# The up-projection of an MLP by Strassen's scheme: seven products of half width in place of eight, in seven of eight groups

## The chip, the cores and the metric

The kernel runs on one core of a Trainium2 chip. The metric is device microseconds (us) of one execution. A measurement takes the median of several runs; the profile is one further execution with the hardware profiler on.

TensorE (PE in the profile) multiplies matrices: a weight load puts a block of 128x128 into the array, then a matmul streams up to 512 columns past it and adds into PSUM. VectorE (DVE) and ScalarE (ACT) work on tiles element by element and can read PSUM; GpSimd (POOL) works on tiles in SBUF; SyncE (SP) issues most of the DMAs. Each engine takes its instructions in order and waits for others on semaphores.

## The reference

A decoder trunk of two layers over 512 tokens of width 1024. Each layer mixes tokens by three attentions, then applies an MLP:

```python
for l in range(DEPTH):
    h = rmsnorm(x, g_mix[l])
...
    x = x + merged @ w_out[l]
    u = rmsnorm(x, g_mlp[l]) @ w_mlp1[l]
    x = x + jnp.square(jax.nn.relu(u)) @ w_mlp2[l]
```

`w_mlp1` is 1024x4096, `w_mlp2` 4096x1024, and everything is float32. The change is in the last two lines.

## The kernel before, in words

All activations are kept transposed, features on the 128 partitions and the 512 tokens along the free axis: x is eight tiles of 128x512 (`s["x"]`), one for each 128 of the 1024 features.

**Three matmuls for one.** A float32 operand is split into a high part (a copy rounded to the matmul's type, by ACT) and a low part (the difference, by DVE): `split_into`, L100 to L102. `mm3` (L108 to L111) adds high times high, high times low and low times high into the same PSUM bank. So each product of a 128x128 weight block and 512 tokens is three matmuls of 512 columns, each with its own weight load.

**The program and its weights.** `layer` builds a list of entries. An entry is a function that issues one piece of work, with the weight units that it needs; a unit is at most 1024 elements on each partition, 512 KB. Behind all layers, the last loop (L926 to L938) walks through the list: before each entry it loads units ahead by SP's queue into `wraw` (3 buffers, `RB`) and splits them into `whi` and `wlo` (4 buffers each, `NB`), in the order in which they are used. A split is one ACT and one DVE instruction of 128x1024 (L101, L102). The framework takes this order as the priority in which it places instructions on the engines, may interleave entries that do not depend on each other, and sets the semaphores.

**The stages of a layer.** Projections and attentions come first, as a planned mix (`PLAN`), then `y8_item` (8 entries), `out_item` (8 entries: the merged output, the addition to x, and `feed`, which scales x by the MLP's gain, splits it into `s["h2"]`, and adds x squared into a running tile), and then the MLP. The factor 1/rms of each token isn't in `h2`: `row_stats` (L241) works it out from the squares, behind the last out item, by small matmuls and a power on POOL, and broadcasts it as `R2` over the partitions. It is applied to u.

**The MLP before.** The 4096 hidden features are four quarters of eight blocks of 128. `u_item(qr, j)` (L833) makes one block: 8 k x 3 matmuls of 512 columns into a bank of `ps_s`, then DVE takes relu times `R2` (L839), ACT squares it twice, once into the high part (L841) and once in place (L842), and DVE subtracts for the low part (L843). `w2_item(qr, ft)` (L847) adds a quarter's share to one of the eight output tiles: 8 k x 3 matmuls into a bank of `ps_acc`, then DVE adds it to x (L853). In the last quarter the output tile is final: it is stored to `out`, or in layer 0 fed to the next layer and stored for it. The order is written out in L902: `u(0) + u(1) + d(0) + u(2) + d(1) + u(3) + d(2) + d(3)`.

**Buffers.** Tiles of 128x512 come from pools: `H` (16) for h, the merged output and the even quarters of u, `O` (16) for `h2` among others, `B` (24) for much in the attentions and the odd quarters of u, `scr` (5) for scratch, `P` (3, of 128x1024) for the attentions' probabilities. PSUM has 2 banks `acc`, 3 `s`, 2 `tp` and 1 `o`.

Of the kernel before, what the change touches and what calls it, by code (L numbers as in the profile page):

```python
# [37 lines left out]


class Entry:  # L40
    def __init__(self, fn, units=()):
        self.fn, self.units = fn, list(units)


def merge(att, gemm):
# [14 lines left out]
def tile_trunk(ctx: ExitStack, tc: tile.TileContext, x_t, mem_t, mem_n, pos, ifr, gcol, grow, w_ck, w_cq, w_kvb, w_qb,  # L60
# [10 lines left out]
    pw_raw, pw_hi, pw_lo = pool("wraw", RB), pool("whi", NB), pool("wlo", NB)  # L71
# [10 lines left out]
    def tl(which, dt=F32):  # L82
        return pools[which].tile([P, 512], dt, tag=which, name=nm(which))
# [197 lines left out]
    def layer(l):  # L281
# [14 lines left out]
        def begin():  # L296
            if l == 0:
                sqs = new_sqs()
                h = []
                xts = []  # L300
                for k in range(KT):
                    xt = tl("X")
                    nc.sync.dma_start(out=xt, in_=x_t[k * P:(k + 1) * P, :])
                    xts.append(xt)
                    if k in (0, 2, 5):
                        load_raw()
                for k, xt in enumerate(xts):
                    h.append(feed(0, k, xt, C_MIX, "H", sqs))
                st["h"], st["sqs"] = h, sqs
            s["h"] = st["h"]  # L310

# [492 lines left out]
        def y8_item(ft):  # L804
            def fn(w):
                q = ps("s")
                for k in range(KT):
                    mm3(q, (w[0][0][:, k, :], w[0][1][:, k, :]), s["od"][k], k == 0, k == KT - 1)
                y_mix(q, 0, ft, False)
                hi, lo = tl("H", F32R), tl("H", F32R)  # L810
# [22 lines left out]
        def u_item(qr, j):  # L833
            def fn(w):
                q = ps("s")
                for k in range(KT):
                    mm3(q, (w[0][0][:, k, :], w[0][1][:, k, :]), s["h2"][k], k == 0, k == KT - 1)
                z = tl("scr")
                V.scalar_tensor_tensor(out=z, in0=q, scalar=0.0, in1=s["R2"], op0=ALU.max, op1=ALU.mult)  # L839
                hi, lo = (tl("H" if qr % 2 == 0 else "B", F32R) for _ in range(2))  # L840
                A.activation(out=hi, in_=z, func=AF.Square)  # L841
                A.activation(out=z, in_=z, func=AF.Square)  # L842
                V.tensor_tensor(out=lo, in0=z, in1=hi, op=ALU.subtract)  # L843
                s.setdefault(("u", qr), []).append((hi, lo))
            return Entry(fn, [w_1[l, qr * 8 + j]])

        def w2_item(qr, ft):  # L847
            def fn(w):
                q = ps("acc")
                for k in range(KT):  # L850
                    mm3(q, (w[0][0][:, k, :], w[0][1][:, k, :]), s["u", qr][k], k == 0, k == KT - 1)
                xt = s["x"][ft]
                V.tensor_tensor(out=xt, in0=q, in1=xt, op=ALU.add)  # L853
                if qr < 3:
                    return
                if l == L - 1:
                    nc.sync.dma_start(out=out[ft * P:(ft + 1) * P, :], in_=xt)
                    return
                if ft == 0:
                    st["sqs"], st["h"] = new_sqs(), []  # L860
                st["h"].append(feed(l + 1, ft, xt, C_MIX, "H", st["sqs"]))
                nc.sync.dma_start(out=xs_dram[ft * P:(ft + 1) * P, :], in_=xt)
            return Entry(fn, [w_2[l, qr, ft]])

        def gy4(w_o, key, b, first):
            r = []
# [33 lines left out]
        u = lambda q: [u_item(q, j) for j in range(8)]  # L900
        d = lambda q: [w2_item(q, ft) for ft in range(KT)]
# [6 lines left out]
    units = [ap for e in prog for ap in e.units]  # L908
    raws, splits = [], []
    consumed = 0  # L910

    def load_raw():
        ap = units[len(raws)]
        a, b = ap.shape[1], ap.shape[2]
        t = pw_raw.tile([P, 1024], F32, tag="wraw", name=nm("wraw"))
        nc.sync.dma_start(out=t[:, :a * b].rearrange("p (a b) -> p a b", a=a), in_=ap)
        raws.append((t, a, b))

    def do_split():
        t, a, b = raws[len(splits)]  # L920
        hi = pw_hi.tile([P, 1024], F32R, tag="whi", name=nm("whi"))
        lo = pw_lo.tile([P, 1024], F32R, tag="wlo", name=nm("wlo"))
        split_into(hi[:, :a * b], lo[:, :a * b], t[:, :a * b])
        splits.append(tuple(z[:, :a * b].rearrange("p (a b) -> p a b", a=a) for z in (hi, lo)))

    for i, e in enumerate(prog):  # L926
        if i == 0:
            e.fn([])
            continue
        while len(splits) < min(len(units), consumed + NB):  # L930
            while len(raws) < min(len(units), len(splits) + RB):
                load_raw()
            do_split()
        while len(raws) < min(len(units), len(splits) + RB):
            load_raw()
        n = len(e.units)
        e.fn(splits[consumed:consumed + n])
        consumed += n  # L938
# [6 lines left out]
def _layout(np, i):  # L945
# [54 lines left out]
    d["w_1"] = each(lambda l: blk(i["w_mlp1"][l], P))  # L1000
    d["w_2"] = each(lambda l: np.stack([blk(i["w_mlp2"][l][q * 1024:(q + 1) * 1024], P) for q in range(4)]))
    return d


# [20 lines left out]
```

## Time and profile before

| | us |
|---|---|
| median of 3 runs (2017.49 to 2018.43) | 2017.84 |
| the profiled execution | 2019.04 |
| its span, first to last instruction | 2017.2 |
| layer 0: start to the end of the out items | 0 to about 667 |
| layer 0: MLP | about 667 to 1017.5 |
| layer 1: MLP | about 1663 to 2017.2 |

How to read it: a page gives the share of the span in which each engine was busy, and the chain of work that ended last, followed back from the last instruction. A group row has line, engine, operation, out<-in by tile names, shapes, count, then busy us in total and mean ns of one, then the idle time before them and what ended it. A window row has busy time and number of instructions of PE, PEld (weight loads), DVE, ACT and POOL in a stretch of the span, then the granted TensorE clock (1.00 is full), the DMA share and GB/s. A timeline row has start, duration, engine, line, operation and tiles. A matmul's duration in it runs to its modelled end and overlaps the next ones; what one costs in a stream is the distance between starts.

### The profile page before, as it was taken

Reading aid. Unit: us, or ns where it says so; the run is one execution under the profiler, and the core shown is the slowest. Engines: PE = TensorE matmul, PEld = TensorE weight load, DVE = VectorE, ACT = ScalarE, POOL = GpSimd, SP = SyncE. Lnnn points to the kernel's source line nnn. Section 1 sums busy time; section 2 is a strip of 40 time slices with the busy share of each in tenths; the row PEclk is TensorE's granted clock in tenths of the full one; section 3 lists DMA queues with packets and bytes.
Section 4 is the critical chain, followed back from the end, with each engine's and each line's share of the span. In section 5 each row is a group of like instructions: output and inputs, shape, how many; then the busy total and the mean of one; then the engine's idle time right before and its main releaser. Section 6 shows DMA issues by size and latency. Waiting matters only on the chain.

```text
span 2017.2 us, 27896 instructions
## 1 busy us (share of the span) xinstructions
PE 1976.3 (98%) x10880; PEld 1711.2 (85%) x10880; DVE 1187.2 (59%) x2235; ACT 961.9 (48%) x1855; POOL 155.7 (8%) x153
## 2 busy tenths in 40 slices
PE   8999999999999999999999999999999999999999
PEld 7778989888888888888888899988888888888887
DVE  7756677687745443434447667678777554434442
ACT  5766765555533432323347667556555333323321
POOL 0300101111100000000002001011111000000000
PEclk9989999999999999999999999999999999999999
DMA  5233222222224333333332321221222333333332
GB/s 170 73 107 105 64 64 69 69 71 66 74 76 149 92 102 94 94 100 100 114 109 65 124 86 53 72 76 63 63 74 74 115 115 94 95 95 101 97 94 73
DMA packets 54676, 181.06 MB, mean 90 GB/s; under 512 B 6417, under 2 KB 7441, under 8 KB 54545
## 3 DMA queue, kind: packets, MB, share of 16 engines
q1 hardware_dynamic: 51840, 175.66, 28.1%
q10 hardware_dynamic: 2704, 3.62, 0.6%
q8 instruction: 86, 1.41, 0.3%
q14 instruction: 46, 0.37, 0.1%
HBM read 175.06 MB, written 4.19 MB: 89 GB/s over the span
## 4 chain that ended last, share of the span: by engine, by line
PE 91%; DVE 5%; ACT 2%; issue 1%; DMA 1%; POOL 0%; ACTq 0%; DVEq 0%; POOLq 0%
PE psacc L109 19%; PE psacc L110 19%; PE psacc L111 19%; PE pss L111 7%; PE pss L109 7%; PE pss L110 7%; PE pss L625 2%; PE pso L654 2%; PE pss L622 2%; PE pstp L666 1%; PE pstp L650 1%; DVE wlo L102 1%; PE pso L110 1%; PE pso L111 1%; PE pso L109 1%
## 5 line engine op out<-in xcount | busy, mean ns | idle before, releaser
L101 ACT ACTIVATE whi<-wraw 128x1024 fp32r<-128x1024 f32 (+3 forms) x320 | 334.4, 1046 | 694.3 <-PE psacc L110 353.8
L102 DVE TENSOR_TENSOR wlo<-wraw,whi 128x1024 fp32r<-128x1024 f32 (+3 forms) x320 | 386.0, 1206 | 94.1 <-ACT whi L101 92.0
L109 PE MATMUL psacc<-H,whi 128*128 128x512 f32 x816 | 321.0, 393 | 3.7 <-DVE G L781 3.2
L110 PE MATMUL psacc<-H,whi 128*128 128x512 f32 x816 | 319.1, 391 | 0.0
L111 PE MATMUL psacc<-H,wlo 128*128 128x512 f32 x816 | 319.0, 391 | 0.0
L109 PE MATMUL psacc<-whi,H 128*128 128x256 f32 (+1 forms) x928 | 270.3, 292 | 11.9 <-ACT whi L101 6.9
L110 PE MATMUL psacc<-wlo,H 128*128 128x256 f32 (+1 forms) x928 | 266.4, 287 | 0.9 <-DVE wlo L102 0.9
L111 PE MATMUL psacc<-whi,H 128*128 128x256 f32 (+1 forms) x928 | 265.5, 288 | 0.0
L110 PE MATMUL pss<-O,whi 128*128 128x512 f32 x640 | 249.2, 389 | 0.0
L111 PE MATMUL pss<-O,wlo 128*128 128x512 f32 x640 | 249.2, 390 | 0.0
L109 PE MATMUL pss<-O,whi 128*128 128x512 f32 x640 | 248.9, 390 | 0.0
L109 PEld LDWEIGHTS psacc<-whi,H 128*128 128x128 f32 x928 | 177.8, 192 | 17.0 <-ACT whi L101 6.9
L109 PEld LDWEIGHTS psacc<-H,whi 128*128 128x128 f32 x816 | 153.3, 188 | 35.7 <-DVE G L781 4.1
L110 PEld LDWEIGHTS psacc<-wlo,H 128*128 128x128 f32 x928 | 178.0, 192 | 3.4 <-DVE wlo L102 1.2
L111 PEld LDWEIGHTS psacc<-H,wlo 128*128 128x128 f32 x816 | 153.3, 188 | 31.8
L110 PEld LDWEIGHTS psacc<-H,whi 128*128 128x128 f32 x816 | 153.3, 188 | 29.9
L111 PEld LDWEIGHTS psacc<-whi,H 128*128 128x128 f32 x928 | 177.2, 192 | 0.3
L853 DVE TENSOR_TENSOR X<-psacc,X 128x512 f32<-128x512 f32 x64 | 44.3, 692 | 207.1 <-PE psacc L111 207.1
L109 PEld LDWEIGHTS pss<-O,whi 128*128 128x128 f32 x640 | 120.2, 188 | 25.7 <-DVE B L792 0.6
L110 PEld LDWEIGHTS pss<-O,whi 128*128 128x128 f32 x640 | 120.2, 188 | 24.9
L639 ACT ACTIVATE P<-pss,nmx 128x128 f32<-128x128 f32 (+2 forms) x224 | 115.5, 521 | 53.9 <-DVE nmx L636 34.7
L111 PEld LDWEIGHTS pss<-O,wlo 128*128 128x128 f32 x640 | 120.2, 188 | 24.7
(233 smaller groups left out, 3291.3 us busy)
## 6 DMA issues: line engine op xcount, KB each, us to landing
wraw<-in_w_dram SPq DMA_DIRECT2D x128, 512.0 KB, 3.6
wraw<-in_w_g_dram SPq DMA_DIRECT2D x48, 512.0 KB, 3.6
wraw<-in_w_d_dram SPq DMA_DIRECT2D x48, 512.0 KB, 3.6
wraw<-in_w_mem_dram SPq DMA_DIRECT2D x16, 512.0 KB, 3.6
wraw<-in_w_od_dram SPq DMA_DIRECT2D x16, 512.0 KB, 3.6
wraw<-in_w_out_dram SPq DMA_DIRECT2D x16, 512.0 KB, 3.8
X<-in_x_t_dram SPq DMA_DIRECT2D x16, 256.0 KB, 4.9
wraw<-in_w_xq_dram SPq DMA_DIRECT2D x8, 512.0 KB, 4.6
```

Source lines behind the costliest of these rows:

```text
L101: A.activation(out=hi, in_=src, func=AF.Copy)
L102: V.tensor_tensor(out=lo, in0=src, in1=hi, op=ALU.subtract)
L109: T.matmul(o, lhsT=l[0], rhs=r[0], start=first, stop=False, **kw)
L110: T.matmul(o, lhsT=l[0], rhs=r[1], start=False, stop=False, **kw)
L111: T.matmul(o, lhsT=l[1], rhs=r[0], start=False, stop=last, **kw)
L622: T.matmul(sw[m][:, :max(N, 256)], lhsT=qk[m][0][i], rhs=qk[m][1], start=i == 0, stop=i == 1)
L625: T.matmul(sv[m], lhsT=qk[m][0], rhs=qk[m][1], start=True, stop=True)
L639: A.activation(out=pt[:, m, :N], in_=sv[m], func=AF.Exp, bias=nmx[:, m:m + 1], accum_out=ssum[m])
L650: T.transpose(tp_[:, j * P:(j + 1) * P], in_=pt[:, 0, j * P:(j + 1) * P], identity=ident)
L654: T.matmul(o, lhsT=w[:, j * P:(j + 1) * P], rhs=vs(j), start=j == 0, stop=j == nb - 1)
L666: T.transpose(tp_[:, i * P:(i + 1) * P], in_=b, identity=ident)
L853: V.tensor_tensor(out=xt, in0=q, in1=xt, op=ALU.add)
```

## The change

A group is now 512 of the 4096 hidden features, in two halves of 256 (n = 0, 1); its weights are four blocks of 512x256: b11 and b12 for the first 512 input features (kh = 0) and the two halves, b21 and b22 for the second 512. The input is cut the same way: a11 and a21 are the first 512 features of the tokens 0 to 255 and 256 to 511, a12 and a22 the second 512 features. Plainly these are eight products of blocks. In seven of the eight groups they become seven, by Winograd's form of Strassen's scheme:

- sums of tokens, once a layer: s1 = a21 + a22, s2 = s1 - a11, s3 = a11 - a21, s4 = a12 - s2 (`mlp_sums`, four calls; ACT scales, DVE adds, then both split them into high and low parts in 16 tiles);
- differences of weights, for each group, on POOL before the split: t1 = b12 - b11, b12 becomes b22 - b12, t2 = b22 - t1, t4 = b21 - t2, the last two written into the raw tile of t1 and t2 once those are split;
- products: "11" a11 b11, "1" s1 t1, "2" s2 t2, "22" a22 t4, "12" a12 b21 (into the bank of "11"), "3" s3 (b22 - b12), "4" s4 b22 (into the bank of "1"). Each is 2 x 4 k x 3 matmuls of 256 columns. ACT copies "11" before "12" adds to it; DVE forms u2 and u3 and the four quarters of the result in two tiles of 128x1024 (c0, c1), and then relu, scale, squares and low parts as before.

Group 0 is done plainly, in four entries of 24 matmuls of 512 columns; `row_stats` and the four `mlp_sums` are issued inside its first two entries. The down-projection is cut into eight groups of four entries, each entry two output tiles with 4 k each (`w2_item(g, fp)`): x is added to eight times instead of four. The products of group g + 1 alternate with the entries of group g. The pool `H` is dropped and `B` has 40 tiles; `wraw` has 5 buffers (`RAW`), `whi` and `wlo` 3 each. The loading loop becomes a list of steps (load, subtract) that runs ahead as far as raw buffers allow. Layouts of `w_1` and `w_2` in memory follow, a unit being 4 KB on each partition as before.

```diff
-    RB, NB = 3, 4
+    RAW, NB = 5, 3
...
-    pools = {n: pool(n, b) for n, b in (("H", 16), ("O", 16), ("X", 8), ("G", 1), ("B", 24), ("scr", 5), ("PT", 4))}
+    pools = {n: pool(n, b) for n, b in (("O", 16), ("X", 8), ("G", 1), ("B", 40), ("scr", 5), ("PT", 4))}
...
-                if ft == KT - 1:
-                    _, _, s["R2"] = row_stats(s["sq2"])
...
+        def mlp_sums(k):
+            ha, hb_ = tl("scr"), tl("scr")
+            scale_to(ha, s["x"][k], col(C_MLP + k))
+            scale_to(hb_, s["x"][k + 4], col(C_MLP + k + 4))
+            a11, a21, a12, a22 = ha[:, :256], ha[:, 256:], hb_[:, :256], hb_[:, 256:]
+            ta, tb = tl("scr"), tl("scr")
+            s1, s2, s3, s4 = ta[:, :256], ta[:, 256:], tb[:, :256], tb[:, 256:]
+            V.tensor_tensor(out=s3, in0=a11, in1=a21, op=ALU.subtract)
+            V.tensor_tensor(out=s1, in0=a21, in1=a22, op=ALU.add)
+            V.tensor_tensor(out=s2, in0=s1, in1=a11, op=ALU.subtract)
+            V.tensor_tensor(out=s4, in0=a12, in1=s2, op=ALU.subtract)
...
+        def u_done(c, n):
+            hl = [(tl("B", F32R), tl("B", F32R)) for _ in range(n)]
+            for i in range(n):
+                A.activation(out=hl[i][0], in_=c[:, i, :], func=AF.Square)
+            A.activation(out=c, in_=c, func=AF.Square)
+            for i in range(n):
+                V.tensor_tensor(out=hl[i][1], in0=c[:, i, :], in1=hl[i][0], op=ALU.subtract)
+            return hl
...
+            def prod(i):
+                def fn(w):
+                    bank = {"11": "X", "12": "X", "22": "Y", "3": "Z", "2": "W", "1": "V", "4": "V"}[i]
+                    new = i not in ("12", "4")
+                    if new:
+                        z[bank] = ps("tp" if bank in "WZ" else "s")
+                    q = z[bank]
+                    for sub in range(2):
+                        for k in range(4):
+                            mm3(q[:, sub * 256:(sub + 1) * 256], (w[0][0][:, k, sub * P:(sub + 1) * P], w[0][1][:, k, sub * P:(sub + 1) * P]), side(i, k),
+                                new and sub == 0 and k == 0, sub == 1 and k == 3, skip_group_check=True)
...
+                    elif i == "3":
+                        z["u3"] = tl("scr")
+                        V.tensor_tensor(out=z["u3"], in0=q, in1=z["u2"], op=ALU.add)
+                        z["c1"] = p_p.tile([P, 2, 512], F32, tag="P", name=nm("c"))
+                        V.tensor_tensor(out=half(z["c1"], 1), in0=v(z["V"]), in1=v(z["u3"]), op=ALU.add)
+                        V.tensor_tensor(out=half(z["c0"], 1), in0=v(z["Y"]), in1=v(z["u3"]), op=ALU.add)
+                        finish(0)
...
+            def finish(j):
+                c = z["c%d" % j]
+                V.scalar_tensor_tensor(out=c, in0=c, scalar=0.0, in1=s["R2"].unsqueeze(1).broadcast_to([P, 2, 512]), op0=ALU.max, op1=ALU.mult)
+                s["u", g, j] = u_done(c, 2)
+            e = [Entry(prod(i), key=(l, g, i)) for i in ("11", "1", "2", "22", "12", "3", "4")]
...
+        def w2_item(g, fp):
...
+                for i in range(2):
+                    ft = 2 * fp + i
+                    q = ps("acc")
+                    for k in range(4):
+                        mm3(q, (w[0][0][:, k, i * P:(i + 1) * P], w[0][1][:, k, i * P:(i + 1) * P]), s["u", g, k // 2][k % 2], k == 0, k == 3)
+                    xt = s["x"][ft]
+                    V.tensor_tensor(out=xt, in0=q, in1=xt, op=ALU.add)
...
-        e += u(0) + u(1) + d(0) + u(2) + d(1) + u(3) + d(2) + d(3)
+        e += u_plain()
+        for g in range(8):
+            d = [w2_item(g, fp) for fp in range(4)]
+            if g == 7:
+                e += d
+                continue
+            u = u_group(g + 1)
+            if g < 6:
+                e += u[:2] + d[:1] + u[2:4] + d[1:2] + u[4:6] + d[2:3] + u[6:] + d[3:]
+            else:
+                e += u[:2] + d[:1] + u[2:6] + d[1:2] + u[6:] + d[2:]
...
+            steps += [("load", b12), ("load", b11), ("sub", t1, b12, b11), ("load", b22), ("into", b12, b22, b12), ("load", b21)]
+            late = [("in", t2, b22, t1), ("in", t4, b21, t2)]
...
+        G.tensor_tensor(out=d["t"], in0=src[0]["t"], in1=src[1]["t"], op=ALU.subtract)
```

More of the change, by code (lines that the diff above doesn't have):

```diff
@@ L40, with __init__ @@
 class Entry:
-    def __init__(self, fn, units=()):
+    def __init__(self, fn, units=(), group=None, key=None):
         self.fn, self.units = fn, list(units)
+        self.group, self.key = group, key
+        self.take = len(self.units) + (key is not None)
 def merge(att, gemm):
@@ L847, in w2_item @@
[L847 to L863, printed above, removed]
+        def mlp_sums(k):
[9 more added lines that the diff above has]
+            V.tensor_tensor(out=s4, in0=a12, in1=s2, op=ALU.subtract)
+            ab = []
+            for t in (ta, tb):
+                hi, lo = tl("B", F32R), tl("B", F32R)
+                split_into(hi, lo, t)
+                ab.append((hi, lo))
+            s.setdefault("S2", []).append(ab)
@@ new lines, in u_plain, with part @@
+        def u_plain():
+            z = {}
+            def part(n, kh):
+                def fn(w):
+                    if kh == 0:
+                        z[n] = [ps("s"), ps("s")]
+                    for sub in range(2):
+                        q = z[n][sub]
+                        sl = slice(sub * P, (sub + 1) * P)
+                        for k in range(4):
+                            mm3(q, (w[0][0][:, k, sl], w[0][1][:, k, sl]), s["h2"][4 * kh + k], kh == 0 and k == 0, kh == 1 and k == 3)
+                    if n == 0:
+                        if kh == 0:
+                            _, _, s["R2"] = row_stats(s["sq2"])
+                        mlp_sums(2 * kh)
+                        mlp_sums(2 * kh + 1)
+                    if kh == 1:
+                        s["u", 0, n] = []
+                        for sub in range(2):
+                            c = tl("scr")
+                            V.scalar_tensor_tensor(out=c, in0=z[n][sub], scalar=0.0, in1=s["R2"], op0=ALU.max, op1=ALU.mult)
+                            s["u", 0, n] += u_done(c.unsqueeze(1), 1)
+                return Entry(fn, [w_1[l, 0, kh, n]])
+            return [part(n, kh) for n in range(2) for kh in range(2)]
@@ L906, in tile_trunk @@
         prog.extend(layer(l))
[L908 to L917, printed above, removed]
-    def do_split():
[L920 to L924, printed above, removed]
+    steps, pieces, sums, late = [], [], {}, []
@@ new lines, in tile_trunk @@
+    for e in prog:
+        if e.group:
+            b11, b12, b21, b22 = ({"ap": ap} for ap in e.group)
+            t1, t2, t4 = {}, {}, {}
+            steps += [("load", b12), ("load", b11), ("sub", t1, b12, b11), ("load", b22), ("into", b12, b22, b12), ("load", b21)]
+            late = [("in", t2, b22, t1), ("in", t4, b21, t2)]
+            sums.update({e.key[:2] + (i,): d for i, d in (("11", b11), ("1", t1), ("2", t2), ("22", t4), ("12", b21), ("3", b12), ("4", b22))})
+        if e.key:
+            pieces.append(sums[e.key])
+        for ap in e.units:
+            d = {"ap": ap}
+            steps.append(("load", d))
+            pieces.append(d)
+        if e.key and e.key[2] in ("1", "2"):
+            steps.append(late.pop(0))
@@ new lines, in tile_trunk, with can_step, prep_step @@
+    last = {}
+    for n, (kind, d, *src) in enumerate(steps):
+        for x in (d, *src):
+            if not (kind == "in" and x is src[1]):
+                last[id(x)] = n
+    at, made, consumed, live = [0], [], 0, [0]
+    def can_step():
+        if at[0] == len(steps):
+            return False
+        kind, d, *src = steps[at[0]]
+        if kind == "in":
+            return "split" in src[1]
+        return kind == "into" or live[0] < RAW
+    def prep_step():
+        kind, d, *src = steps[at[0]]
+        at[0] += 1
+        if kind in ("load", "sub"):
+            d["t"] = pw_raw.tile([P, 1024], F32, tag="wraw", name=nm("wraw"))
+            live[0] += 1
+        if kind == "load":
+            a, b = d["ab"] = d["ap"].shape[1], d["ap"].shape[2]
+            nc.sync.dma_start(out=d["t"][:, :a * b].rearrange("p (a b) -> p a b", a=a), in_=d["ap"])
+            return
+        if kind == "in":
+            d["t"] = src[1]["t"]
+            live[0] += 1
+        d["ab"] = src[0]["ab"]
+        G.tensor_tensor(out=d["t"], in0=src[0]["t"], in1=src[1]["t"], op=ALU.subtract)
@@ L926, in tile_trunk @@
+    def do_split():
+        d = pieces[len(made)]
+        (a, b), t = d["ab"], d["t"]
+        n = a * b
+        hi, lo = (pw.tile([P, 1024], F32R, tag=k, name=nm(k)) for pw, k in ((pw_hi, "whi"), (pw_lo, "wlo")))
+        split_into(hi[:, :n], lo[:, :n], t[:, :n])
+        made.append(tuple(z[:, :n].rearrange("p (a b) -> p a b", a=a) for z in (hi, lo)))
+        d["split"] = True
+        live[0] -= 1
     for i, e in enumerate(prog):
```

80 lines of the change are left out of this document (52 added, 28 removed).

## The prediction

> **What bounds the kernel now.** The page comes first: busy times and the chain that ended last.
>
> ```profile
> span 2017.2 us, 27896 instructions
> ...
> PE 1976.3 (98%) x10880; PEld 1711.2 (85%) x10880; DVE 1187.2 (59%) x2235; ACT 961.9 (48%) x1855; POOL 155.7 (8%) x153
> ...
> PE 91%; DVE 5%; ACT 2%; issue 1%; DMA 1%; POOL 0%; ACTq 0%; DVEq 0%; POOLq 0%
> ```
>
> The chain is 91% matmuls, so TensorE's stream sets the end. Busy time overlaps between matmuls and hides gaps, so the windows by stage come next: DVE diff attention of layer 0, then its MLP.
>
> ```profile
> 300.00:560.00 260.00, 251.78 (x1673) 228.95 (x1672) 196.28 (x456) 145.51 (x328) 39.73 (x37) 1.00 0.23 70
> ...
> 667.00:1017.50 350.50, 350.50 (x1556) 290.39 (x1555) 152.59 (x177) 114.32 (x145) 1.01 (x1) 1.00 0.33 101
> ```
>
> In the MLP PE is busy throughout (350.50 of 350.50) at clock 1.00, DVE 44%, ACT 33%, POOL nearly never. Only the number of matmuls times the distance between their starts counts there. That distance is read from two timelines: a first and a 37th matmul of 512 columns (MLP), and a first and a 67th of 256 columns (memory projection), nothing between but matmuls of the same shape.
>
> ```profile
> 899.84 0.39 PE L109 MATMUL pss<-O,whi 128*128 128x512 f32 x1
> ...
> 908.00 0.39 PE L109 MATMUL pss<-O,whi 128*128 128x512 f32 x1
> ```
>
> ```profile
> 154.76 0.28 PE L109 MATMUL psacc<-whi,O 128*128 128x256 f32 x1
> ...
> 162.68 0.28 PE L109 MATMUL psacc<-whi,O 128*128 128x256 f32 x1
> ```
>
> 8.16 us over 36 steps is 226.7 ns; 7.92 us over 66 steps is 120.0 ns. Half the columns cost 53%, each with a weight load of its own. Break-even for seven products against eight quarters is 96 x 226.7 / 168 = 129.5 ns.
>
> **TensorE's term.** For 512 hidden columns the plain up-projection takes 4 outputs x 8 k x 3 = 96 matmuls of 512 columns, 21.76 us. Seven products take 7 x 2 x 4 x 3 = 168 of 256, 20.16 us. That is 1.60 us less; with 7 groups in 2 layers, 22.4 us less. The down-projection keeps its 768 matmuls a layer, the first group its 96. A rule speaks against this: the Trainium skill (TensorE: Matmul & The Clock Gate, Back-to-back issue gap) gives sustained spacings of about 81 ns at 128 columns and 131 ns at 512; halfway by columns, an estimate of 98 ns at 256, seven products would cost 3.9 us more a group. The trace has 226.7 and 120.0 ns and disagrees.
>
> **What the group adds beside it.** Prices of the other engines, by shape:
>
> ```profile
> L102 DVE TENSOR_TENSOR wlo<-wraw,whi 128x1024 fp32r<-128x1024 f32 x306 | 374.2, 1223 | 91.2 <-ACT whi L101 89.3 <-PE psacc L111 1.1 <-PE pstp L424 0.4
> L101 ACT ACTIVATE whi<-wraw 128x1024 fp32r<-128x1024 f32 x306 | 323.8, 1059 | 671.8 <-PE psacc L110 342.0 <-PE pss L110 213.9 <-issue 65.3
> ...
> L853 DVE TENSOR_TENSOR X<-psacc,X 128x512 f32<-128x512 f32 x64 | 44.3, 692 | 207.1 <-PE psacc L111 207.1
> ...
> L842 ACT ACTIVATE scr<-scr 128x512 f32<-128x512 f32 x64 | 40.6, 634 | 2.1
> ...
> L589 DVE TENSOR_TENSOR scr<-scr,ra 128x256 f32<-128x256 f32 x64 | 24.6, 415 | 0.2
> ...
> L843 DVE TENSOR_TENSOR B<-scr,B 128x512 fp32r<-128x512 f32 x32 | 22.1, 692 | 0.1
> ...
> L574 ACT ACTIVATE scr<-psacc 128x512 f32<-128x512 f32 x32 | 19.1, 597 | 26.1 <-PE psacc L111 26.0
> ```
>
> DVE per group: 11 splits (7 products, 4 down) x 1.223 = 13.5; u2, u3 and three halves from PSUM 5 x 0.692 = 3.5; two relu-and-scale passes of 1024 priced like the split, 2.4; four low parts x 0.692 = 2.8; eight additions to x, now of half the depth and so twice as many, 5.5: 27.7 us beside 168 x 0.120 + 96 x 0.2267 = 41.9 us of PE. ACT: 11 x 1.059 + 2 x 0.597 + 4 x 0.634 + 2 x 1.059 = 17.5 us. Both fit.
>
> POOL gets four subtractions of 1024 a group, an operation that before does not show at that size. Its nearest rows, and what they show of meeting DVE (minimum/median/maximum ns):
>
> ```profile
> L292 POOL TENSOR_TENSOR ra<-cosd,gr x8: 448/462/910, 53.5 to 535.6; 128x128 f32<-128x128 f32 x8
> ```
>
> ```profile
> L293 POOL TENSOR_TENSOR rb<-nsind,gr x4: 449/484/1442, 52.3 to 532.4; 128x128 f32<-128x128 f32 x4
> ```
>
> ```profile
> L591 DVE TENSOR_TENSOR scr<-scr,scr x32: 664/682/891, 227.1 to 1527.1; 128x512 f32<-128x512 f32 x32
> ```
>
> ```profile
> 532.28 1.28 DVE L102 TENSOR_TENSOR wlo<-wraw,whi 128x1024 fp32r<-128x1024 f32 x1
> ```
>
> ```profile
> 532.44 1.44 POOL L293 TENSOR_TENSOR rb<-nsind,gr 128x128 f32<-128x128 f32 x1
> ```
>
> ```profile
> L182 POOL COPY am<-cosd 128x64 f32<-128x64 f32 x1 | 0.2, 233 | 0.0
> ```
>
> Bounds: 0.46 us if width were free, 8 x 0.462 = 3.7 us if it all scales. I take the copy's 0.23 as the fixed part and 0.23 for each 128 columns: 2.1 us, between the ends and built from the nearest rows. By a page alone, the Trainium skill (GPSIMD Engine Reference, Performance versus the Vector engine), 4497 ns at 2048 columns, the estimate is 2.25 us. In the pair of rows at 532 us POOL's subtraction started 0.16 us into DVE's and ended 0.32 us behind it, 1.44 instead of 0.45: the later one waits. The Trainium skill (SBUF — State Buffer, Who interferes with whom) says the same of a DVE operation with two SBUF inputs against a GpSimd read, and the trace agrees. So I count POOL's 4 x 2.1 = 8.4 us as blocking DVE in full: 36.1 of 41.9, still not the bound.
>
> The new waits are on buffers. Weights have 3 split buffers instead of 4, so a split may start when the unit three back is done, and two units are left: at least two products, 5.76 us, for 1.06 + 1.22 = 2.29 us on ACT and DVE. t2 and t4 are subtracted only once t1 and t2 are split; counted from the end of the unit that frees t2's buffer, its split, POOL's 2.1 and t4's split make 6.7 us, where one product, the down item, and another product, 11.2 us, stand ahead of t4's use. Loads (64 a layer as before) keep SP's queue:
>
> ```profile
> wraw<-in_w_dram SPq DMA_DIRECT2D x128, 512.0 KB, 3.6
> ```
>
> The slot of a raw weight is empty at least 5.5 us before what is loaded into it next is used (the tightest: the first half of t1, between the split of product "3" and that of the third down unit), and a load lands in 3.6. Behind a late subtraction on POOL stands the next one and, once a layer, the power of the token sums, whose row is
>
> ```profile
> L134 POOL TENSOR_TENSOR r<-ms,mhalf 128x4 f32<-128x4 f32 x4 | 4.9, 1220 | 553.3 <-ACT O L412 352.9 <-DVE ms L244 200.4
> ```
>
> and which nobody needs before the first plain output is complete, 10.9 us in. So I put the groups at 0; their bound is rival (b).
>
> **Seams.** The rows of a feed, which each out item and each last down item ends with:
>
> ```profile
> L105 ACT ACTIVATE H<-X,gc 128x512 fp32r<-128x512 f32 x16 | 11.4, 711 | 0.2 <-DVE X L853 0.2
> ```
>
> ```profile
> L106 DVE SCALAR_TENSOR_TENSOR H<-X,gc,H 128x512 fp32r<-128x512 f32 x16 | 12.0, 748 | 1.1 <-ACT H L105 0.9
> ...
> L229 DVE TENSOR_TENSOR scr<-scr,scr 128x512 f32<-128x512 f32 x28 | 19.2, 685 | 0.1
> ```
>
> From the first plain unit to product "1", which needs all S sums, PE has 96 x 0.2267 + 2.88 = 24.6 us. DVE must do in it four sums at 4 x 0.415 + 2 x 0.692 = 3.04, 12.2 us; four splits 4.9; the plain group's first half 4 x 0.692 = 2.8; the last out item 0.692 + 0.748 + 0.685 = 2.1 and small statistics, estimated 0.4: 22.4 us. (ACT: four sums at 2 x 0.711 + 2 x 0.634, 10.8, and some 9 of the rest.) If the sums overlap, 0 late; if each runs alone through ACT and DVE (two scalings, four sums, two casts and a low part: 1.42 + 1.66 + 1.27 + 0.69 = 5.0 us), then 2.5 for the out item, 20.1 for the sums and 7.7 for the rest stand against 24.6, 5.7 late. DVE is nine tenths full and the scratch buffers couple the sums: I take 1.0, nearer the full-overlap end because splits and sums may interleave. Two layers: +2.0.
>
> At the layer seam, the last group's outputs now end twice as often. The first and the tenth matmul behind the seam, and all of PE's waits for split weights:
>
> ```profile
> 1017.48 0.29 PE L109 MATMUL psacc<-whi,H 128*128 128x288 f32 x1
> ...
> 1018.66 0.29 PE L109 MATMUL psacc<-whi,H 128*128 128x288 f32 x1
> ```
>
> ```profile
> PE psacc L109 <- ACT whi L101: 6.9, 1, 6.9
> ...
> PE psacc L110 <- DVE wlo L102: 0.9, 1, 0.9
> ```
>
> An item of two outputs wants 2 x (0.692 + 0.748 + 0.685) + 1.223 = 5.47 us of DVE in 5.44 of PE. Two accumulators absorb 2.7 us; the next layer's first matmuls (131 ns apart, 12 a k) need the last h only 11 us in. That item holds all three split buffers, so the next unit is split only when its first part is done, 3 us in, and still 9 us ahead of its use. 0 to 3; I take +1.0. In the attention stages the fourth buffer is gone. PE waited for split weights twice in the whole run, 6.9 and 0.9 us, and the shortest units there are 24 matmuls of 120 ns: cover 5.76 again. A new schedule may gain as well as lose: -2 to +5, I take +1.0. The end is unchanged, one addition (0.692) and one store.
>
> Sum: -22.4 + 2.0 + 1.0 + 1.0 = -18.4. The profiled execution took 2019.04 us, 1.84 outside its span; that gives 2000.6. It lay 1.2 above the median of 2017.84, so **1999.4 us**. Its own range: -24.4 (seams free, attention -2) to -3.0 (5.7 twice, 3, 5), 1993 to 2015.
>
> **Rivals.** (a) The sums come late: no overlap, 5.7 a layer, with 3 at the layer seam: -22.4 + 11.4 + 3 + 1 = -7, 2011. For it: DVE's 22.4 of 24.6 us. Against: sums need only x, ready before.
> (b) Slower: POOL's subtraction holds DVE and splits come late in every group. A down unit has 5.76 - 2.29 = 3.47 us to spare; a subtraction at 3.7 and two low parts (1.4) in front make 5.1, 1.6 late. Two of the three down units that follow two products so: 3.2 lost against 1.6 won, 14 x 1.6 = +22, with +4 for the seams 2044. It decides from 1.6 us a group; at 2.1 us a subtraction the delay is 3.5 and just hidden. For it: the pair at 532 us. Against: POOL is idle most of the time and the first of two goes.
> (c) The shorter matmul costs more here: at the 131 ns of the 288-column rows, 22.0 against 21.76, +3.5, with +4 for seams 2025. Against: 67 rows at 120.0. The spacings of the issue-gap section named above point this way.
> (d) Attention loses with three buffers: +9 instead of +1, 2007. For it: DVE 75% busy there. Against: the two waits.
>
> **Chances.** Forecast 0.70, (a) 0.12, (b) 0.09, (c) 0.04, (d) 0.05. 0.2% is 4 us, about what a measurement can tell. Faster: forecast, (a), (d), 0.87; slower 0.08 from (b) and (c); the same 0.05, from the rest of (b) and (c) near their break-even. The range runs from 1993 to 2012: most of the forecast, (a) and (d).
>
> **What would show it.** Right: 256-column products 120 ns apart with no PE idle inside a group, 83.9 us for two groups with their eighths; DVE near 66% there; POOL's subtractions near 2 us. Wrong: PE waiting for whi or wlo before down units (b); PE waiting for split S tiles at the first "1" (a); starts over 129 ns apart (c); attention stages longer than before (d).

## The result, and the profile after

The changed kernel took 1999.28 us (median of 4 runs, 1998.37 to 1999.83) where the kernel before took 2018.13 beside it (4 runs, 2017.49 to 2019.21): ratio 0.9906, 95% interval 0.9888 to 0.9923. The prediction was 1999.4. Its profiled execution took 1999.83 us. The page after, span, busy times and chain:

```profile
span 1998.0 us, 30334 instructions
...
PE 1956.1 (98%) x11888; PEld 1739.9 (87%) x11888; DVE 1352.1 (68%) x2431; ACT 1029.5 (52%) x1929; POOL 305.6 (15%) x209
...
PE 90%; DVE 5%; ACT 2%; issue 1%; DMA 1%; ACTq 0%; DVEq 0%
```

There are 1008 more matmuls (11888 against 10880) and 20 us less of PE. The chain is TensorE's as before; DVE went from 59% to 68%, POOL from 8% to 15%. The window over layer 0's MLP, busy times of PE, PEld, DVE, ACT, POOL:

```profile
667.00:1003.00 336.00, 335.57 (x2044) 301.75 (x2044) 228.44 (x269) 146.98 (x180) 74.61 (x28) 1.00 0.33 104
```

PE lacks 0.43 us of being full there, all of it in one place (below). To split the time by stage I take one mark in both kernels: the sixth addition of the out items, and the last addition of the down-projection, once a layer. First the timeline of before, then of after (start, duration):

```profile
656.67 0.69 DVE L827 SCALAR_TENSOR_TENSOR X<-psacc,X 128x512 f32<-128x512 f32 x1 [2.03 <-PE psacc L111]
...
1017.68 0.69 DVE L853 TENSOR_TENSOR X<-psacc,X 128x512 f32<-128x512 f32 x1 [2.33 <-PE psacc L111]
...
1652.52 0.69 DVE L827 SCALAR_TENSOR_TENSOR X<-psacc,X 128x512 f32<-128x512 f32 x1 [2.04 <-PE psacc L111]
...
2013.50 0.69 DVE L853 TENSOR_TENSOR X<-psacc,X 128x512 f32<-128x512 f32 x1 [4.75 <-PE psacc L111]
```

```profile
655.25 0.69 DVE L829 SCALAR_TENSOR_TENSOR X<-psacc,X 128x512 f32<-128x512 f32 x1 [2.03 <-PE psacc L113]
...
1008.15 0.69 DVE L947 TENSOR_TENSOR X<-psacc,X 128x512 f32<-128x512 f32 x1 [0.15 <-PE psacc L113]
...
1643.51 0.69 DVE L829 SCALAR_TENSOR_TENSOR X<-psacc,X 128x512 f32<-128x512 f32 x1 [2.03 <-PE psacc L113]
...
1994.38 0.69 DVE L947 TENSOR_TENSOR X<-psacc,X 128x512 f32<-128x512 f32 x1 [2.03 <-PE psacc L113]
```

Layer 0's MLP is 361.01 us before and 352.90 after, but after holds 16 matmuls of the next layer, before 2, at 0.131 us each. Without them:

| us | before | after | difference |
|---|---|---|---|
| layer 0, up to the mark | 656.67 | 655.25 | -1.4 |
| layer 0, MLP | 360.74 | 350.81 | -9.9 |
| layer 1, up to the mark | 635.10 | 637.45 | +2.35 |
| layer 1, MLP | 360.99 | 350.87 | -10.1 |

Within the MLP, the first down matmul behind the first two products, in one group and in the group three later, and the first and last of two products in a row between them (48 matmuls), from the timeline of after:

```profile
749.28 0.40 PE L111 MATMUL psacc<-B,whi 128*128 128x512 f32 x1
...
875.28 0.40 PE L111 MATMUL psacc<-B,whi 128*128 128x512 f32 x1
```

```profile
754.75 0.28 PE L111 MATMUL pss<-O,whi 128*128 128x256 f32 x1
...
760.38 0.28 PE L113 MATMUL pstp<-B,wlo 128*128 128x256 f32 x1
```

126.00 us for three groups is 42.00 a group, and 5.63 us over 47 steps is 119.8 ns a product matmul. A window over nearly two groups, in which PE is full, so that no group waits for anything:

```profile
720.00:803.70 83.70, 83.70 (x529) 76.08 (x528) 54.00 (x61) 33.46 (x38) 22.05 (x8) 1.00 0.32 100
```

DVE is at 54.00 of 83.70, 65%. The one wait of the MLP lies in the plain group, with what DVE and POOL did before it:

```profile
683.90 0.39 PE L113 MATMUL pss<-O,wlo 128*128 128x512 f32 x1
684.72 0.50 PE L111 MATMUL pss<-O,whi 128*128 128x512 f32 x1 [0.43 <-DVE scr L888]
```

```profile
672.04 2.39 POOL L1055 TENSOR_TENSOR wraw<-wraw,wraw 128x1024 f32<-128x1024 f32 x1 [6.30 <-DMA wraw<-in_w_dram]
```

```profile
671.36 0.69 DVE L104 TENSOR_TENSOR B<-scr,B 128x512 fp32r<-128x512 f32 x1 [0.24 <-ACT B L103]
672.16 2.56 DVE L840 TENSOR_TENSOR scr<-scr 128x256 f32<-128x256 f32 x1
...
683.98 0.68 DVE L888 SCALAR_TENSOR_TENSOR scr<-pss,R 128x512 f32<-128x512 f32 x1
```

One start is 0.82 us behind the last instead of 0.227: 0.59 us lost (0.46 in layer 1). Three of the four plain outputs fill the three banks of `ps_s`. The wait comes 72 matmuls into the group, where the fourth needs a bank, and the bank comes free with the plain close of DVE (L888: relu and scale of a plain output), which comes late in DVE's queue of sums. One of the sums (L840) took 2.56 us: it started 0.12 us into a weight difference of POOL and ended 0.29 us behind it. The other sums of that line in this layer take 0.42. Such a stretch, in which DVE stands behind POOL, is called a hold below.

### The profile page after: what moved, and what is told of

Its sections match the earlier page's. It is cut to its first block, busy times and chain, and to the rows that moved or that the text cites. A ratio compares the mean times of both kernels' runs of the same rounds, so it can differ in the third digit from the quotient of the medians.

```text
span 1998.0 us, 30334 instructions
## 1 busy us (share of the span) xinstructions
PE 1956.1 (98%) x11888; PEld 1739.9 (87%) x11888; DVE 1352.1 (68%) x2431; ACT 1029.5 (52%) x1929; POOL 305.6 (15%) x209
## 4 chain that ended last, share of the span: by engine, by line
PE 90%; DVE 5%; ACT 2%; issue 1%; DMA 1%; ACTq 0%; DVEq 0%
PE psacc L111 20%; PE psacc L112 20%; PE psacc L113 20%; PE pss L113 5%; PE pss L111 5%; PE pss L112 5%; PE pss L627 2%; PE pso L656 2%; PE pss L624 1%; PE pstp L113 1%; PE pstp L112 1%; PE pstp L111 1%; PE pstp L668 1%; DVE wlo L104 1%; PE pstp L652 1%
## 5 line engine op out<-in xcount | busy, mean ns | idle before, releaser
L103 ACT ACTIVATE whi<-wraw 128x1024 fp32r<-128x1024 f32 (+1 forms) x362 | 378.7, 1047 | 522.6 <-PE psacc L112 225.0
L104 DVE TENSOR_TENSOR wlo<-wraw,whi 128x1024 fp32r<-128x1024 f32 (+1 forms) x362 | 444.6, 1228 | 126.1 <-ACT whi L103 124.4
L111 PE MATMUL psacc<-B,whi 128*128 128x512 f32 x1072 | 421.2, 393 | 2.7 <-DVE G L783 2.7
L112 PE MATMUL psacc<-B,whi 128*128 128x512 f32 x1072 | 419.5, 391 | 0.0
L113 PE MATMUL psacc<-B,wlo 128*128 128x512 f32 x1072 | 418.6, 390 | 0.0
L111 PE MATMUL psacc<-whi,B 128*128 128x256 f32 (+3 forms) x1008 | 302.0, 300 | 14.7 <-ACT whi L103 6.9
L112 PE MATMUL psacc<-wlo,B 128*128 128x256 f32 (+3 forms) x1008 | 295.5, 293 | 1.2 <-DVE wlo L104 1.2
L113 PE MATMUL psacc<-whi,B 128*128 128x256 f32 (+3 forms) x1008 | 293.4, 292 | 0.0
L1055 POOL TENSOR_TENSOR wraw<-wraw,wraw 128x1024 f32<-128x1024 f32 x56 | 152.7, 2726 | 572.0 <-DVE wlo L104 501.9
L111 PEld LDWEIGHTS psacc<-B,whi 128*128 128x128 f32 x1072 | 201.6, 188 | 42.9 <-DVE G L783 3.5
L113 PEld LDWEIGHTS psacc<-B,wlo 128*128 128x128 f32 x1072 | 201.4, 188 | 42.2
L112 PEld LDWEIGHTS psacc<-B,whi 128*128 128x128 f32 x1072 | 201.6, 188 | 37.8
L111 PEld LDWEIGHTS psacc<-whi,B 128*128 128x128 f32 x1008 | 192.9, 192 | 22.7 <-ACT whi L103 6.9
L113 PEld LDWEIGHTS psacc<-whi,B 128*128 128x128 f32 x1008 | 192.6, 192 | 1.7
L111 PE MATMUL pss<-O,whi 128*128 128x256 f32 (+1 forms) x528 | 170.2, 323 | 1.6 <-ACT whi L103 0.9
L112 PE MATMUL pss<-O,whi 128*128 128x256 f32 (+1 forms) x528 | 170.3, 322 | 0.0
```

The source lines that it names most:

```text
L103: A.activation(out=hi, in_=src, func=AF.Copy)
L104: V.tensor_tensor(out=lo, in0=src, in1=hi, op=ALU.subtract)
L111: T.matmul(o, lhsT=l[0], rhs=r[0], start=first, stop=False, **kw)
L112: T.matmul(o, lhsT=l[0], rhs=r[1], start=False, stop=False, **kw)
L113: T.matmul(o, lhsT=l[1], rhs=r[0], start=False, stop=last, **kw)
L1055: G.tensor_tensor(out=d["t"], in0=src[0]["t"], in1=src[1]["t"], op=ALU.subtract)
```

## The experiments

Theory: the gain is the product stream alone; small losses lie in the plain group (sums on DVE, held by POOL) and ahead of it (three split buffers). Rivals: the gain comes from something else in the change, or it is smaller than the scheme gives because POOL or the order of the entries holds the groups back. Each time stands beside runs of the kernel before in the same session: 2018.46 us in the first, 2019.19 in the second, 2017.93 in the third.

**All eight groups plain.** Token sums and weight differences go with the products; four plain entries alternate with four down entries. The rest of the change, buffers and eighths too, stays.

```diff
-            u = u_group(g + 1)
...
+            u = u_plain(g + 1)
+            for a, b in zip(u, d):
+                e += [a, b]
```

> All eight groups plain (96 matmuls of 512 columns each, no token sums, no weight differences), everything else of the changed kernel kept: three split buffers, five raw ones, one pool B, down-projection in eighths alternating with the plain entries. Theory (the gain is the matmul stream, the rest costs about nothing): the 2 x 7 groups give back 14 x (96 x 226.7 - 168 x 119.8) ns = 23 us, less the 1.2 us that the two seams with sums cost: 1999.3 + 22 = 2021, a little over the kernel before. Rival (part of the gain comes from the rearrangement, buffers or alternation): clearly below before, at 2005 to 2013.

2020.77 us (10 runs), ratio 1.0010 (1.0000 to 1.0019); the MLPs 360.73 and 360.92, before's to 0.1 us. That is 21.5 us over the changed kernel's 1999.28 (another session), beside 14 x 1.53 = 21.4 from the product stream. The whole gain is the seven products.

**Weight differences on VectorE.**

```diff
-        G.tensor_tensor(out=d["t"], in0=src[0]["t"], in1=src[1]["t"], op=ALU.subtract)
+        V.tensor_tensor(out=d["t"], in0=src[0]["t"], in1=src[1]["t"], op=ALU.subtract)
```

> The four weight differences of a group run on VectorE (about 1.22 us each) instead of GpSimd (2.73). Theory (TensorE sets the end and both engines have cover): VectorE 27.7 + 4.9 = 32.6 of 41.9 us a group, no more waits, time within 2 us of 1999.3; the instructions that GpSimd delayed in the seam (sums of 256 columns 0.94 us, low parts 1.07 us) fall back to 0.42 and 0.69. Rival (GpSimd's length or its hold on VectorE costs time): faster by 2 to 10 us. Rival (VectorE is near its limit): slower by over 5 us.

1994.94 us (1992.52 to 1998.41), ratio 0.9884 (0.9866 to 0.9903): 4.3 under the changed kernel, which is more than the theory allowed and in the range of the first rival. But its MLPs are 350.33 and 350.50, only 0.85 less in all; the wait in the plain group is gone, and the sums' line no longer has a long one:

```profile
L840 DVE TENSOR_TENSOR scr<-scr x8: 416/422/426, 667.5 to 1665.3; 128x256 f32<-128x256 f32 x8
```

The same two groups, and the group row of the differences:

```profile
720.00:803.70 83.70, 83.70 (x529) 76.07 (x528) 61.81 (x69) 33.49 (x38) 0.00 (x0) 1.00 0.31 101
```

```profile
L1055 DVE TENSOR_TENSOR wraw<-wraw,wraw 128x1024 f32<-128x1024 f32 x56 | 68.4, 1221 | 2.3 <-DMA wraw<-in_w_dram 1.4
```

DVE took over 8 differences of 1.22 us, 9.8, and its busy time grew by 7.8: beside POOL it had lost about 2.0 us in two groups to holds, 0.25 a difference. The remaining 3.4 us of the gain are ahead of the MLPs, in stages whose code is the same. One part is seen: a wait of PE in layer 1 that this version's order of instructions does not have, in the timeline of the changed kernel:

```profile
1441.28 0.47 PE L624 MATMUL pss<-B,B 128*128 128x256 f32 x2 [1.86 <-DVE B L608]
```

Its starts are 2.0 us further apart than the shape's usual distance. The run with four pairs below has the differences on DVE too and shows this wait again, so it goes with the order in which the instructions were placed, not with the engine. To see whether the 4.3 us were chance, both kernels were run again, the changed one in the second session:

> The changed kernel as it is, once more on another chip or the same, beside the others. Theory (the 4.3 us by which the weight differences on VectorE came out ahead are 1.1 us of the seams and otherwise half-clock stretches of TensorE in the attention stages that differ from execution to execution): 1997 to 2000.5 us, with a before of 2018.4. Rival (a steady cost of the subtractions on GpSimd that the trace does not show): 1999.3 with no execution under 1998.4.

It gave 1998.32 us (1996.35 to 2003.41), ratio 0.9901 (0.9888 to 0.9915); executions under 1998.4 refute a steady 1999.3. In the third session both were run:

> The changed kernel as it is, beside the version with the differences on VectorE in the same session: by both theories 1997 to 2000.5 us; what counts is its distance to the other, 1.5 to 4 us by the theory and under 1 us by the rival.

> The version with the weight differences on VectorE once more, beside the changed kernel in the same session. Theory (seams 1.0 us shorter, a 2.0 us wait at 1439 us in the second layer's attention gone with the other order of instructions, the rest by the number of half-clock stretches): 1.5 to 4 us under the changed kernel run beside it, 1993.5 to 1997. Rival (the first session's 4.3 us were the spread of executions alone): within 1 us of the changed kernel run beside it.

1997.70 (1995.34 to 2002.55) for the changed kernel, 1993.66 (1991.88 to 1995.05) for the differences on DVE, ratios 0.9904 (0.9891 to 0.9918) and 0.9879 (0.9863 to 0.9894). The distance is 4.0 us again, and here the two ranges do not overlap, so it is not chance. It is the best version tried. About 0.9 (MLPs) and 2.0 (the wait in layer 1) are located. The rest goes with TensorE's granted clock: it averages 0.9975 over the 13 executions of the changed kernel and 0.9988 over the 8 of this version, and at the same 0.999 their means are 1996.6 and 1993.9, only 2.7 apart (the last section has more on this clock).

**POOL's work doubled.** A second pass over each difference, times one.

```diff
+        G.tensor_tensor(out=d["t"], in0=d["t"], in1=ones.broadcast_to([P, 1024]), op=ALU.mult)
```

> Each weight difference is followed on GpSimd by a second pass of the same size over it (times one), so GpSimd works 4 x 5.45 = 21.8 us a group. Theory (a later one waits, but splits have cover): the longest chain, split t2, difference t4, split t4, grows from 7.3 to 10.0 us of the 11.2 in front of its use, so 0 to 14 us slower than 1999.3 (0 to 1 us a group). Rival (GpSimd holds VectorE for its whole length): VectorE would need 27.7 + 21.8 = 49.5 of 41.9 us a group, 7.6 late, over 100 us slower.

2009.16 us (2006.11 to 2011.37), ratio 0.9952 (0.9937 to 0.9966). POOL is busy 42.73 us in the two groups, twice as much, and PE lost only 0.3 us there, although DVE's holds in them grew from about 2.0 to 8.5 us (60.51 less the 52.0 that DVE needs without differences):

```profile
720.00:803.70 83.70, 83.38 (x523) 75.48 (x522) 60.51 (x60) 32.18 (x37) 42.73 (x17) 1.00 0.31 101
```

The 10 us are mostly in the plain group, where two DVE operations now wait for POOL, PE waits long for the same bank, and TensorE's clock falls behind the wait (a window; the clock is the column behind POOL):

```profile
671.48 2.52 DVE L840 TENSOR_TENSOR scr<-scr 128x256 f32<-128x256 f32 x1
673.92 2.91 DVE L104 TENSOR_TENSOR wlo<-wraw,whi 128x1024 fp32r<-128x1024 f32 x1
```

```profile
685.70 0.50 PE L111 MATMUL pss<-O,whi 128*128 128x512 f32 x1 [2.95 <-DVE scr L888]
```

```profile
682.00:691.00 9.00, 6.05 (x20) 4.52 (x19) 7.06 (x15) 6.09 (x11) 0.00 (x0) 0.81 0.18 58
```

So it is mostly in this one place, once a layer, that POOL's hold reaches PE, and there the wait grows with it (0.43 to 2.95 us). The time lies in the theory's range, but not by the theory's mechanism, which had the loss inside the groups.

**No token sums.**

```diff
-                        mlp_sums(2 * kh)
-                        mlp_sums(2 * kh + 1)
...
-                     "1": (ss[0], a), "2": (ss[0], b), "3": (ss[1], a), "4": (ss[1], b)}[i]
+                     "1": (h[k], b), "2": (h[k + 4], a), "3": (h[k + 4], b), "4": (h[k], a)}[i]
```

> The changed kernel without the tokens' sums: products 1, 2, 3 and 4 take plain halves of the tokens in place of the sums, so the result is another and the sum's 8 scalings, 16 VectorE operations and 8 splits per layer are left out. All products keep their number and size. Theory of the forecast (product 1 waits for the sums, 1.0 us per layer): no PE wait of over 0.2 us between the first plain unit and the first product of a group, 2.0 us less than after, 1997.3. Reading of the trace of after (the sums stand on VectorE ahead of the plain close, so that a PSUM bank comes free 0.59 and 0.46 us late, and the weight subtractions hold VectorE meanwhile): the same place is free of the wait, 1.05 us less, 1998.2. Rival (the wait comes from the row statistics or the subtractions, not from the sums): the wait stays within 0.1 us, 1999.3. The time alone can't tell 1 us; the seam's waits in the trace do.

1999.38 us (1996.43 to 2000.95), not told apart from the changed kernel by time. By the trace: no wait left in the plain group, MLPs 350.07 and 350.26, 1.35 us less in all. Taking away the sums, or moving the differences from POOL to DVE, removes the same wait. So it needs a DVE queue full of sums and something more that delays it; POOL's hold is one such thing, and the run with four pairs below shows another.

**The seven products in a row, then the four down units.**

```diff
-            if g < 6:
-                e += u[:2] + d[:1] + u[2:4] + d[1:2] + u[4:6] + d[2:3] + u[6:] + d[3:]
...
+            e += u + d
```

> The seven products of a group follow each other, then the four down entries; nothing else changes. Theory (VectorE's 27.7 us fit into 41.9 on average only because products and down entries alternate): in the 20.2 us of products VectorE must do seven splits 8.6 and closings 8.7, up to 10.9 us more if GpSimd holds it, and the differences t2 and t4 stand two products apart instead of a product, a down entry and a product: TensorE waits 2 to 8 us a group, 28 to 110 us slower. Rival (the average load decides, order does not matter): within 3 us of 1999.3.

2002.92 us (1999.77 to 2004.98), ratio 0.9920 (0.9906 to 0.9935). The expected 28 to 110 us did not come; the rival's 3 us are nearer. Beside the wait in the plain group, PE waits only in the first group of products, right behind the sums:

```profile
698.27 0.39 PE L111 MATMUL pss<-O,whi 128*128 128x256 f32 x1 [0.40 <-ACT whi L103]
699.62 0.39 PE L113 MATMUL pss<-O,wlo 128*128 128x256 f32 x1 [0.85 <-DVE wlo L104]
```

The MLPs are 352.52 and 352.60, 1.7 each over the alternating order; in every later group PE stays full, so seven products alone (20.2 us) leave DVE enough time. The alternation is worth little beyond the first group.

**Before with the new buffers alone.**

```diff
-    RB, NB = 3, 4
+    RB, NB = 5, 3
...
```

> The kernel before with the changed kernel's buffers alone: five raw weight buffers instead of three, three pairs of split weights instead of four, pools H and B made one of 40. No product is changed. Theory of the forecast (attention loses about 1.0 us in all with the new buffers, bounds -2 to +5): 2019.4 us beside a before of 2018.4, so a difference of -2 to +5. Reading of the trace of after: only the eight products ahead of the out items wait for a split that comes late, 1.6 us per layer, so +3.2 and 2021.6. Rival (d) of the forecast (three pairs starve the attention stages, -18.4 of the sum becomes 2007): +8.6, 2027. What tells: the waits of the weight load on the ScalarE split in these items, and the attention stages' length by the addition marks (656.7 and 635.1 us in before).

2017.29 us (11 runs, 2015.90 to 2020.39), ratio 0.9997 (0.9988 to 1.0006): no loss that can be measured, and the 8.6 us of rival (d) are refuted. A wait is there all the same, ahead of the out items, in the changed kernel as here. The timeline of the changed kernel, PE and then ACT:

```profile
593.99 0.39 PE L112 MATMUL pss<-O,whi 128*128 128x512 f32 x1
594.59 0.50 PE L111 MATMUL pss<-O,whi 128*128 128x512 f32 x1 [0.21 <-ACT whi L103]
594.92 0.40 PE L112 MATMUL pss<-O,whi 128*128 128x512 f32 x1
595.54 0.50 PE L111 MATMUL pss<-O,whi 128*128 128x512 f32 x1 [0.22 <-ACT whi L103]
```

```profile
592.53 2.96 ACT L103 ACTIVATE whi<-wraw 128x1024 fp32r<-128x1024 f32 x3 [1.62 <-PE pss L112]
```

Three `y8_item` entries stand open side by side until the last `od` tile comes; each holds a pair of split weights. With three pairs none is left, and the next three splits start only when the open items end, together. What that costs is read from the first matmul of these items to the mark. In before, and then in the changed kernel:

```profile
592.94 0.48 PE L109 MATMUL pss<-O,whi 128*128 128x512 f32 x1
```

```profile
589.94 0.48 PE L111 MATMUL pss<-O,whi 128*128 128x512 f32 x1
```

The marks lie 63.73 and 65.31 us behind, so three pairs cost about 1.57 us here. It is the same in layer 1, and so in every run with three pairs, this one too. So 3.1 us of waits were added here and the time did not grow: something else in the attention stages made up for it. A part is the granted clock, on average 0.9977 against 0.9970 of before beside it; the rest is not known. The waits of the weight loads:

```profile
PEld pss L111 <- ACT whi L103: 3.5, 6, 0.7
```

All the runs with three pairs have them; before and the next run, both with four pairs, do not.

**Four pairs of split weights, and pool B of 36 to make room**, on the version with the differences on DVE.

```diff
-    RAW, NB = 5, 3
+    RAW, NB = 5, 4
...
-    ... ("B", 40) ...
+    ... ("B", 36) ...
```

> The weight differences on VectorE as in the second experiment, and four pairs of split weights instead of three (pool B 36 instead of 40 to make room). Theory: a fourth pair takes the waits on the late split out of the items ahead of the out items (1.6 us per layer in the runs with three pairs), so 3.2 us less than the 1994.9 of the second experiment: 1991.7 (1990 to 1994). Rival: the smaller pool B (36) makes the up-projection's squares wait for buffers that the down items still hold, PE stalls of over 1 us per group inside the MLP, 14 us or more slower, 2009. Rival: the waits only move to the next item, nothing won, 1994.9.

2023.49 us (11 runs), ratio 1.0022 (1.0013 to 1.0031). The waits above are gone, as the theory said, and 28 us were lost elsewhere: only 0.6 us in each MLP (350.97 and 351.09), the rest before the marks, which stand at 668.51 and 645.00 us. The first rival looked for the loss in the MLP, the second expected none. The 0.6 us is the wait of the plain group, back without any difference on POOL: here a difference on DVE itself stands among the sums, ahead of the plain close.

```profile
694.58 1.22 DVE L1055 TENSOR_TENSOR wraw<-wraw,wraw 128x1024 f32<-128x1024 f32 x1
```

```profile
698.06 0.50 PE L111 MATMUL pss<-O,whi 128*128 128x512 f32 x1 [0.51 <-DVE scr L888]
```

To tell pool from pairs, pool B of 36 with three pairs:

> As the version with the differences on VectorE, three pairs of split weights, but pool B of 36 instead of 40: the smaller half of what the run with four pairs changed. That run was 28 us over, all of it in the attention stages (668.5 and 645.0 us against 653.3 and 635.1). Theory (the smaller pool B makes the attention's projections wait for buffers, as the 11.6 us wait of a first matmul shows): 2015 to 2025. Rival (the fourth pair moved the splits into other engines' way): 1994 to 1998.

2023.02 us (8 runs), ratio 1.0025 (1.0015 to 1.0035), marks 673.86 and 642.99: it is the pool, so the first rival had the cause right and the place wrong. The largest single wait, on PE, on ACT, and in a window:

```profile
159.82 0.58 PE L111 MATMUL psacc<-whi,O 128*128 128x256 f32 x1 [12.10 <-ACT O L107]
```

```profile
159.26 1.71 ACT L107 ACTIVATE O<-B,gc 128x256 fp32r<-128x256 f32 x4 [2.28 <-DMA B<-in_mem_t_dram]
```

```profile
150.00:170.00 20.00, 10.18 (x67) 10.18 (x68) 5.09 (x12) 7.51 (x17) 0.70 (x1) 0.66 0.27 87
```

The memory's tokens are loaded into pool B, late (from 156.3 us on, with pool B of 40 from 134.6), and TensorE waits 12 us. Its clock is at half from 151 to 164.5 us, through most of the wait and 4.7 us behind it. These are some 12 of the 29 us by which this run is over the version with pool B of 40; where the others lie was not followed.

## Why the prediction was right, point by point

**TensorE's term, -22.4.** Right to 1 us. The products cost what was taken, 120.0 ns (119.8). A group takes 42.00 us where 41.9 was the sum, against 192 x 0.2267 = 43.53 before; 14 x 1.53 is -21.4. The missing 0.08 us a group is in the four down units (5.47 us from the first matmul of one to the first product behind it, where 5.44 was taken). The 98 ns that the prediction estimates for 256 columns from two spacings is called halfway by columns; it is a third of the way from 128 to 512. The measured 119.8 ns is above it either way.

**Groups, 0.** Right: a period of 42.00 us and no wait. DVE's 27.7 us a group was 27.0, ACT's 17.5 was 16.7. POOL's difference was taken as 2.1 us:

```profile
L1055 POOL TENSOR_TENSOR wraw<-wraw,wraw x56: 2390/2589/3318, 662.9 to 1935.9; 128x1024 f32<-128x1024 f32 x56
```

It takes 2.39 us when nothing meets it, 2.59 at the median. Counting all of it as blocking DVE was far too much: about 0.25 us of each. The 2.1 us itself, built from a fixed and a growing part, was 0.3 too little.

**Seams, +2.0 for the sums.** The size is half (0.59 + 0.46 = 1.05 by PE's waits, 1.35 by the run without sums), and the step itself failed: product "1" does not wait for the sums. What waits is a plain unit, for its PSUM bank, and POOL's hold at the wrong moment is part of it. The prediction looked for the first reader of the sums; it counted the plain closes among DVE's load, but not that the last plain output waits for the first of them, which stands among the sums in DVE's queue.

**Layer seam, +1.0.** Wrong, 0: no PE wait stands there. Matmuls of the next layer's first k, 16 of them, were put among the last down units; that this is the reason is argued, not shown.

**Attention, +1.0.** In the profiled executions -1.4 + 2.35 = +0.95, but this sum is no proof: that it met the +1.0 is luck, since effects of other sizes cancel. The three pairs cost 1.57 us a layer, 3.1 us; the argument "cover 5.76 us" failed because units are not used up one at a time. And TensorE had 13.6 us at half clock there in before, 10.2 in after; taking half of it off, an estimate, leaves 1284.9 and 1287.6 us, +2.6. That the new buffers alone gave 1287.0 by the same estimate (3.4 us at half clock) fits. Why this is less than the 3.1 us of the pairs, and why the wait at 1441 us does not add to it, was not followed.

**The sum.** -21.4 + 1.05 + 0.95 = -19.4 against -19.2 between the spans (2017.2 and 1998.0); the prediction had -18.4. TensorE's term carries it; that the forecast time came within 0.2 us of the measured one owes something to luck, since of the three small terms one was half, one was nothing, and one was met by cancelling.

**The rivals.** (a) No product waited for the sums. (b) Refuted with room to spare: POOL at double the work costs the groups 0.3 us in 84, not the 3.2 that its break-even asked for; 42 of the 56 differences start when DVE has just ended a split (by the releasers of line L1055), which may be why so little meets; that reason is argued, not shown. (c) 119.8 ns, not 131. (d) Refuted by the buffers alone; the run with pool B of 36 shows that these stages can be starved of buffers, in another pool.

## What to carry to other kernels

Where a window shows TensorE full and its clock at 1.00, count matmuls times the measured distance of starts at each width: that term alone made the forecast. For everything beside it, walk each in-order queue past the moved work and ask what else stands in it (here a plain close between sums), and count buffers by the items that can be open at once, not by units used per item. A second engine is not free help: here the differences were 0.9 us better in the MLPs on the busier engine, DVE, which had the time and then was held by no one.

## What the runs showed of the hardware

Two things were not expected. The hold between POOL and DVE is seen as a DVE operation of 2.56 us for 0.42 that ends just behind POOL's; the Trainium skill (SBUF — State Buffer, Who interferes with whom) says that a DVE instruction with two SBUF inputs contends with a GpSimd instruction that reads SBUF, and that the ports they share are an exclusive lock, and this row agrees. Yet its total is small here: about 2.0 us in two groups with eight differences.

TensorE's clock drops in the middle of the run. In before:

```profile
130.00:150.00 20.00, 17.12 (x81) 14.35 (x82) 12.49 (x31) 17.24 (x46) 0.70 (x1) 0.74 0.32 104
```

The granted clock goes to half for 3.41 us or a few times that (10.2 us before this kernel's first mark), in the attention stages, around 130 to 155, 453 and 1437 to 1456 us, each of them in several runs, where PE waits often. Which of them occur differs from one execution to the next: the changed kernel had 10.2, 10.2 and 0 us before its first mark, 655.25, 654.93 and 650.76 us long. It goes with most of the spread of some 8 us between executions of one kernel: of the changed kernel's 13, the four with a granted clock of 0.999 took 1995.3 to 1997.7 us, the five with 0.997 1999.0 to 2000.7, the one with 0.995 2003.4. Behind the 2.95 us wait above, and its like in layer 1, such a stretch stands in the MLP as well, where no other run has one. The Trainium skill (TensorE: Matmul & The Clock Gate, What's actually happening) tells of an idle window of about 3.4 us after which the clock is halved; the stretches' lengths agree, but shorter waits sufficed here, sometimes. In before, a wait of 1.44 us and the window behind it:

```profile
1451.61 0.39 PE L109 MATMUL psacc<-whi,H 128*128 128x256 f32 x1 [1.44 <-ACT B L562]
```

```profile
1452.90:1456.40 3.50, 3.50 (x19) 3.50 (x18) 0.76 (x2) 0.29 (x1) 0.00 (x0) 0.51 0.00 0
```

The same wait of 1.44 us in the changed kernel, at 1443.19 us, has no such stretch behind it. In the traces of all 13 profiles TensorE was idle for 1.5 to 3.2 of the 3.41 us ahead of each stretch, the one at the end of the run left aside. A small wait on TensorE can so cost some 1.7 us more than itself for each 3.41 us at half clock, an estimate (half of the stretch).
